# Latent-attention queries normed, split and projected between the last gate products; the sample recurrence in two buffers

## The chip, the cores and the metric

The kernel runs on one core of one Trainium2 chip. The metric is the time of one execution on the device in microseconds, here the median of three runs. The engines are TensorE (PE, matrix products; PEld is its weight load), VectorE (DVE), ScalarE (ACT), GpSimd (POOL) and SyncE (SP), which here only issues transfers.

## What is computed

One decoder layer on 1024 prompt tokens and 8 sample tokens (NT = 1032), width 1024. The input is modulated and projected once (`h @ w_in`); the columns feed a recurrence (RWKV-7), a latent attention (MLA) and two gates. The two branches are merged through the gates, then a norm and a layer of 64 routed experts follow. All of it is in float32. The part that the change touches:

```
h    = x * (1 + sc1) + sh1
proj = h @ w_in                  # 1792 rwkv | 384 q_low | 256 kv_low | 32 kr_low | 2048 gates
cq   = rmsnorm(q_low,  g_qnorm)
q    = (cq @ w_uq).reshape(b, t, 8, 64 + 32)
q_nope, q_rope = q[..., :64], rope(q[..., 64:], pos)
ckv  = rmsnorm(kv_low, g_kvnorm)          # an output too
k_rope = rope(kr_low, pos)                # one for all 8 heads, an output too
k_nope = ckv @ w_uk ; v = ckv @ w_uv      # per head
o_b  = causal softmax((q_nope k_nope + q_rope k_rope) * scale) v
# sample tokens, one step of the recurrence for each (state S, 8 heads of 64 x 64):
sa = S (-kk) ; S = S * w + sa (kk a)^T + v k^T ; o = S r
```

The last row of the rwkv columns of every sequence (`shift`) and the new S are outputs.

## The kernel before

Products in float32 are made of three: each operand is split in a hi part (a rounded copy, ScalarE) and a lo part (the rest, VectorE), and `mm3` issues hi x hi, lo x hi and hi x lo (lines 147 to 149). `split` (lines 1312 and 1315) makes the two parts. Activations lie with features on the partitions and tokens along the free axis, in chunks of 344 (`CH`).

The program is written with a tile framework: code order gives the dependences, pools with a number of buffers hold the tiles, and a scheduler puts the instructions on each engine in an order of its own that respects both. Each engine, and SP as a queue of transfers, goes through its list in order. An instruction that waits holds all behind it on its engine.

Around the change the stages are these.

1. `stage_b`, then `mla_in` (line 488): `win` projects 128 columns of `w_in` at a time, 72 products of 128x344 each, for q0, q1, q2, kv0, kv1 and kr. `mla_weights` (line 870) loads the rope tables, w_uq, w_uk and w_uv.
2. The gates. `gate` (line 331) projects 128 gate columns, writes them to DRAM (gateD) and adds four small `psada` products whose weights wada come in 1 MB loads. While g8 to g15 run, `mla_in` norms q and kv (square, a product with ones `psq`, root, reciprocal, scaling), and `rw_sample` (line 775) does the recurrence for the sample tokens: for four pairs of heads it loads the state sS and a broadcast of the inputs svb, both in one buffer and on POOL's queue, does nine VectorE steps and writes S back.
3. `mla_prep` (line 1050) in a pool of its own: `shift_out`, then the splits of the normed q (qp0 to qp2) and kv (kvp0, kvp1), w_uk and w_uv; `mla_rope` for two sets of four heads (products psqr; the halves of each head are swapped by a write to and a read from DRAM, swapD, and combined with the cosines and sines); `mla_k` (rope of the key, the ckv and krope rows by transposes psck); `mla_heads` for four pairs (q products psqn, k products pskn; each head's q and k as one 128-row tile, written to qD and kD); `mla_v` (psV, written to vD); `sample_queries` (psuk, psql, psqrs) and `rw_sample_rows` (psos).
4. `mla_prompt` (line 1086): for four pairs of heads it loads Va, and for each head qTa and kTa in one load each, and runs eight query tiles (sc scores, pspt transposes, pspv). The chunked recurrence of the prompt (`rwkv`) is interleaved with it. Output products, norm and experts follow.

Of the kernel before, what the change touches and what calls it, by code (L numbers as in the profile page):

```python
# [126 lines left out]
class Kern:  # L127
# [241 lines left out]
    def shift_out(self, pool):  # L369
        nc = self.nc  # L370
        so = pool.tile([9, 1792], F32, tag='ss', name='so', bufs=1)
        for g in range(4):
            n = min(4, 14 - g * 4)
            ps = self.ps(f'psso{g}')
            for j in range(n):
                self.tr(ps[:9, j * 128:(j + 1) * 128], self.plast[:, g * 4 + j, :])
            nc.scalar.activation(so[:, g * 512:g * 512 + n * 128], ps[:9, :n * 128], AF.Copy)
        nc.scalar.dma_start(self.O['shift_prompt'][0], so[0:1, :])
        nc.scalar.dma_start(self.O['shift_sample'][0], so[1:9, :])
# [108 lines left out]
    def mla_in(self, pool, keep):  # L488
        nc = self.nc
        T = lambda nm: keep.tile([128, NT], F32, name=nm)  # L490
        q = [self.win([(1792 + i * 128, 128)], f'q{i}', T(f'cq{i}')) for i in range(3)]
        kv = [self.win([(2176 + i * 128, 128)], f'kv{i}', T(f'ck{i}')) for i in range(2)]
        kr = self.win([(2432, 32), (2448, 16), (2432, 16)], 'kr', T('krraw'))
        self.epsr = self.cp.tile([128, 1], F32, name='epsr')
        nc.vector.memset(self.epsr, 1e-6)
        for tl, nm in ((q, 'g_qnorm'), (kv, 'g_kvnorm')):
            self.gate()
            rs = pool.tile([128, NT], F32, tag='rs', name='rs' + nm, bufs=1)
            sqs = []
            for t in tl:  # L500
                sq = pool.tile([128, NT], F32, tag='sq', name='sqm', bufs=3)
                nc.scalar.activation(sq, t, AF.Square)
                sqs.append(sq)
            for c0, n in CH:
                ps = self.ps('psq')
                for j, sq in enumerate(sqs):
                    nc.tensor.matmul(ps[:, :n], self.c('ones'), sq[:, c0:c0 + n], start=(j == 0), stop=(j == len(tl) - 1))
                nc.scalar.activation(rs[:, c0:c0 + n], ps[:, :n], AF.Sqrt, bias=self.epsr, scale=1.0 / (128 * len(tl)))
# [1656 lines left out]
def layer(tc, I, O, dbg=None):  # L2165
    nc = tc.nc
    with ExitStack() as ctx:
# [3 lines left out]
        with ExitStack() as b:  # L2171
# [14 lines left out]
            with sb('proj') as B:  # L2186
                K.stage_b(B)
# [111 lines left out]
```

## Time and profile before

| | us |
|---|---|
| median of 3 runs (2512.29 to 2514.46) | 2513.09 |
| the profiled execution | 2506.96 |
| its span | 2505.1 |
| stage 2, g8 to g15 with norms and sample recurrence | about 428 to 538 |
| stage 3, `mla_prep` | about 538 to 664 |
| stage 4, attention and prompt recurrence | about 664 to 1010 |
| TensorE busy over the span | 2165.5 (86%) |
| VectorE, ScalarE, GpSimd busy | 1422.0, 978.8, 972.0 |

Times in the rows are microseconds from the start of the span. The profile names tiles without their numbers: whg and wlg are the hi and lo parts of a gate's weights, g a gate, cq and ck the raw and then the normed q and kv columns. A row of the timeline is one instruction, or several of the same kind in sequence, with its start and its duration; matrix products overlap, so the step between two starts is the price of one, not the duration. The waits are given by who waited, for whom, the sum, the number and the longest.

### The profile page before, as it was taken

The numbers are of one execution on the slowest core, as the hardware profiler recorded it, in microseconds if no ns is written. First come the engines' busy times: TensorE is split into PE (matmuls) and PEld (weight loads), VectorE is DVE, ScalarE is ACT, GpSimd is POOL, SyncE is SP. The second block draws the span as 40 slices with busy tenths as digits, with TensorE's granted clock in tenths as the row PEclk, the third lists the DMA queues.
The fourth block names the chain that finished last, engine by engine and source line by source line (L and its number), as shares of the span: only waits on it lengthen the run. The fifth ranks groups of instructions, "written<-read, shape, count | busy, mean of one in ns | idle before, by whom it ended". The sixth has DMA issues, their size and how long they took to land. (4 is left out here: it accounts for less than half of the span.)

```text
span 2505.1 us, 39711 instructions
## 1 busy us (share of the span) xinstructions
PE 2165.5 (86%) x14376; PEld 1721.5 (69%) x14376; DVE 1422.0 (57%) x2637; ACT 978.8 (39%) x1722; POOL 972.0 (39%) x813
## 2 busy tenths in 40 slices
PE   4999999976799999799779688899999998799754
PEld 2898999865567878467768476576767767676331
DVE  1554441553476775554657865676666667575437
ACT  1433332322354454321326643444443444344325
POOL 2443340132300000320214765567576665565226
PEclk8999999987898999899899789899999999999877
DMA  8136662654551442654899669999999999899994
GB/s 281 45 79 173 178 185 56 181 160 135 199 161 32 147 128 73 246 192 135 278 236 226 146 154 273 317 310 323 326 307 313 308 303 340 245 312 292 319 316 159
DMA packets 353203, 537.86 MB, mean 215 GB/s; under 512 B 113467, under 2 KB 210178, under 8 KB 346652
## 3 DMA queue, kind: packets, MB, share of 16 engines
q1 hardware_dynamic: 288602, 415.90, 50.9%
q0 software_dynamic: 61520, 118.93, 19.9%
q8 instruction: 114, 1.87, 0.3%
q10 hardware_dynamic: 2882, 0.48, 0.1%
q14 instruction: 85, 0.70, 0.1%
HBM read 411.00 MB, written 124.77 MB: 214 GB/s over the span
## 5 line engine op out<-in xcount | busy, mean ns | idle before, releaser
L1794 POOL DMA_INDIRECT xg<-h2D,IG x303 | 353.3, 1166 | 242.1 <-DVE xt L1797 81.0
L1315 DVE TENSOR_TENSOR epl<-egu,eph 128x1024 fp32r<-128x1024 f32 x140 | 169.7, 1218 | 123.0 <-ACT eph L1312 122.6
L1312 ACT ACTIVATE eph<-egu 128x1024 fp32r<-128x1024 f32 x140 | 147.3, 1056 | 165.9 <-DMA egu<-in_w_exp_up_dram 102.7
L147 PE MATMUL psup<-xh,eph 128*128 128x360 f32 (+15 forms) x576 | 182.1, 325 | 21.9 <-ACT xh L1312 18.6
L149 PE MATMUL psup<-xh,epl 128*128 128x360 f32 (+15 forms) x576 | 178.3, 322 | 10.8 <-DVE epl L1315 10.0
L148 PE MATMUL psup<-xl,eph 128*128 128x360 f32 (+15 forms) x576 | 182.8, 320 | 4.0 <-DVE xl L1315 3.9
L1934 POOL DMA_INDIRECT accD<-ey,IS x65 | 115.2, 1773 | 112.8 <-ACT ey L1927 55.8
L147 PE MATMUL psy<-edh,ehh 128*128 128x512 f32 (+12 forms) x296 | 126.0, 432 | 23.7 <-ACT ehh L1312 11.4
L1315 DVE TENSOR_TENSOR edl<-ewd,edh 128x1024 fp32r<-128x1024 f32 x90 | 108.7, 1219 | 45.0 <-ACT edh L1312 44.3
L147 PEld LDWEIGHTS psup<-xh,eph 128*128 128x128 f32 x576 | 111.1, 195 | 31.7 <-ACT xh L1312 20.2
L1312 ACT ACTIVATE edh<-ewd 128x1024 fp32r<-128x1024 f32 x90 | 94.0, 1052 | 82.6 <-PE psy L149 67.2
L147 PE MATMUL pwg<-hh,whg 128*128 128x344 f32 x384 | 124.1, 323 | 0.0
L149 PEld LDWEIGHTS psup<-xh,epl 128*128 128x128 f32 x576 | 109.6, 194 | 19.9 <-DVE epl L1315 11.6
L148 PE MATMUL pwg<-hl,whg 128*128 128x344 f32 x384 | 122.6, 319 | 0.0
L149 PE MATMUL pwg<-hh,wlg 128*128 128x344 f32 x384 | 122.6, 319 | 0.0
L148 PE MATMUL psy<-edl,ehh 128*128 128x512 f32 (+12 forms) x296 | 120.9, 413 | 0.0
L148 PEld LDWEIGHTS psup<-xl,eph 128*128 128x128 f32 x576 | 111.5, 194 | 9.7 <-DVE xl L1315 5.4
L1797 DVE STREAM_TRANSPOSE xt<-xg 128x1024 f32<-128x1024 f32 (+3 forms) x61 | 113.9, 1873 | 0.2
L149 PE MATMUL psy<-edh,ehl 128*128 128x512 f32 (+12 forms) x296 | 109.9, 414 | 0.9 <-DVE ehl L1315 0.8
L1873 PE MATMUL psup<-xf,egu 128*128 128x176 f32 (+7 forms) x640 | 96.2, 304 | 2.7 <-DMA egu<-in_w_exp_gate_dram 2.1
L1873 PEld LDWEIGHTS psup<-xf,egu 128*128 128x128 f32 x640 | 91.6, 190 | 7.2 <-DMA egu<-in_w_exp_gate_dram 3.3
L1947 PE MATMUL psup<-egu,xf 128*32 128x128 f32 (+1 forms) x1024 | 77.1, 325 | 21.2 <-DMA egu<-in_w_exp_up_dram 16.9
(731 smaller groups left out, 5879.4 us busy)
## 6 DMA issues: line engine op xcount, KB each, us to landing
egu<-in_w_exp_gate_dram SPq DMA_DIRECT2D x256, 256.0 KB
egu<-in_w_exp_up_dram SPq DMA_DIRECT2D x256, 256.0 KB
ewd<-in_w_exp_down_dram SPq DMA_DIRECT2D x128, 512.0 KB
wada<-in_w_ada_dram SPq DMA_DIRECT2D x24, 1024.0 KB
accD<-zero SPq DMA_DIRECT2D x18, 512.0 KB
gateD<-g SPq DMA_DIRECT2D x16, 516.0 KB
bg<-gateD SPq DMA_DIRECT2D x48, 172.0 KB
wrg<-in_w_in_dram SPq DMA_DIRECT2D x16, 512.0 KB
```

What stands on the lines that cost most here:

```text
L147: nc.tensor.matmul(out, lh, rh, start=start, stop=False)
L148: nc.tensor.matmul(out, lh, rl, start=False, stop=False)
L149: nc.tensor.matmul(out, ll, rh, start=False, stop=stop)
L1312: nc.scalar.activation(hi, src, AF.Copy)
L1315: self.last_split = nc.vector.tensor_sub(lo, src, hi.bitcast(F32))
L1794: nc.gpsimd.indirect_dma_start(out=X[:, g, :], out_offset=None, in_=h4, in_offset=bass.IndirectOffsetOnAxis(ap=idx(j, g), axis=0))
L1797: nc.vector.transpose(out=dst.rearrange("p k (g b) -> p g k b", b=32), in_=X[:, 0:G, :].rearrange("p g (a k) -> p g k a", k=8))
L1873: nc.tensor.matmul(p[:, :C], gu[k // 2][:, j, k % 2, m * 128:(m + 1) * 128], xt[:, k, :C], start=(k == 0), stop=(k == 7))
L1934: self.nc.gpsimd.indirect_dma_start(out=acc, in_=y, in_offset=None, compute_op=OP.add, out_offset=bass.IndirectOffsetOnAxis(ap=idx, axis=0))
L1947: nc.tensor.matmul(ps[q * C:q * C + C, 0:2 * F].rearrange("p (a f) -> p a f", a=2), xt[:, k, :C], gu[k // 2][:, :, k % 2, q * F:q * F + F] ...
```

## The change

The banks of PSUM are split into five for the projections and three (`mq`) for the new work, after `stage_b`. The rest:

- `rw_sample` becomes `rw_sample_load` and one call for each pair of heads. sS and svb have two buffers. Their loads and the writes to sD go on SP's queue (they were on POOL's and ScalarE's). Pairs 0 and 1 are written between the q and the kv projections, 2 and 3 before g9.
- `mla_norm` goes by chunks of 344 and for q makes the hi and lo parts at once.
- `mla_rope`, `mla_q`, `mla_kr`, `mla_rows` and `shift_out` stand between g10 and g15. One pool of 8 buffers of 128x344 (tag `n`) serves all of them. The swap through DRAM is made for each chunk. Results go to DRAM as qnD (4 pairs of 128 rows), qrotD and krD. `shift_out` takes seven groups with 14 transfers on SP for two on ScalarE.
- `mla_prep` keeps the kv parts, kn and V and the sample queries. w_uk and w_uv are loaded there; they were loaded in stage 1.
- `mla_prompt` puts each head's q and k together from four loads: 64 rows of qnD, 32 of qrotD, 64 of knD, and the 32 rows of krD twice by a broadcast. 32 rows of q are set to zero by POOL.

```diff
...
+    def mla_in(self, qpool, keep, between):
...
+        self.mq = [self.win([(1792 + i * 128, 128)], f'q{i}', T(qpool, f'cq{i}')) for i in range(3)]
+        between()
+        self.mkv = [self.win([(2176 + i * 128, 128)], f'kv{i}', T(keep, f'ck{i}')) for i in range(2)]
+        self.mkr = self.win([(2432, 32), (2448, 16), (2432, 16)], 'kr', T(keep, 'krraw'))
...
+    def ntile(self, pool, nm):
+        return pool.tile([128, 344], F32, tag='n', name=nm, bufs=8)
+    def mla_norm(self, tl, nm, pool, parts=None):
+        nc = self.nc
+        for c0, n in CH:
+            s = slice(c0, c0 + n)
+            ps = self.ps('psq', 'mq')
             for j, t in enumerate(tl):
+                sq = self.ntile(pool, 'sqm')
+                nc.scalar.activation(sq[:, :n], t[:, s], AF.Square)
+                nc.tensor.matmul(ps[:, :n], self.c('ones'), sq[:, :n], start=(j == 0), stop=(j == len(tl) - 1))
+            rs = self.ntile(pool, 'rs' + nm)
+            nc.scalar.activation(rs[:, :n], ps[:, :n], AF.Sqrt, bias=self.epsr, scale=1.0 / (128 * len(tl)))
+            nc.vector.reciprocal(rs[:, :n], rs[:, :n])
+            for j, t in enumerate(tl):
+                nc.vector.scalar_tensor_tensor(t[:, s], t[:, s], self.v(nm, j), rs[:, :n], op0=OP.mult, op1=OP.mult)
+                if parts:
+                    self.split(parts[j][0][:, s], parts[j][1][:, s], t[:, s])
...
+    def rw_sample(self, hp, pool):
...
+        S = pool.tile([128, 8, 64], F32, tag='sS', name='sS', bufs=2)
+        V = pool.tile([128, 5, 8, 64], F32, tag='svb', name='svb', bufs=2)
+        for hh in range(2):
+            nc.sync.dma_start(S[hh * 64:hh * 64 + 64], I['state_wkv'][0, :, 2 * hp + hh].rearrange("b v k -> v b k"))
+            nc.sync.dma_start(V[hh * 64:hh * 64 + 64].rearrange("p j b k -> p (j b k)"),
+                              self.sD[hp, hh:hh + 1].rearrange("o j b k -> o (j b k)").to_broadcast([64, 2560]))
...
+        for hh in range(2):
+            nc.gpsimd.dma_start(self.O['wkv_sample'][0, :, 2 * hp + hh].rearrange("b v k -> v b k"), S[hh * 64:hh * 64 + 64])
...
     def orow(self, dt):
...
     def mla_rope(self, X, pool):
+            ps = self.ps('psqr', 'mq')
+            for k in range(3):
+                self.mm3(ps[:, :n], [w[:, k, X, :, :].rearrange("p a b -> p (a b)") for w in self.wqr],
+                         [t[:, s] for t in self.qp[k]], k == 0, k == 2)
+            t0, t1, t2 = [self.ntile(pool, f'qr{j}')[:, :n] for j in range(3)]
+            nc.scalar.activation(t0, ps[:, :n], AF.Copy)
+            nc.vector.tensor_mul(t1, ps[:, :n], self.cosT[:, s])
+            d = self.dr.tile([4, 4, 16, n], F32, name=f'swapD{X}{c0}')
             for j in range(2):
+                nc.sync.dma_start(d[:, 2 * j:2 * j + 2], t0)
+            nc.sync.dma_start(t2, d[:, 1:3])
+            nc.gpsimd.tensor_mul(t2, t2, self.sinT[:, s])
+            nc.gpsimd.tensor_add(t1, t1, t2)
+            nc.sync.dma_start(self.qrotD[X][:, s], t1)
+            if c0 + n == NT:
+                nc.gpsimd.tensor_copy(self.qrot[:, X, :], t1[:, NP - c0:])
+    def mla_q(self, hp, pool):
...
+        for c0, n in CH:
+            s = slice(c0, c0 + n)
+            ps = self.ps('psqn', 'mq')
+            for k in range(3):
+                self.mm3(ps[:, :n], [w[:, k, hp * 128:(hp + 1) * 128] for w in self.wqn], [t[:, s] for t in self.qp[k]],
+                         k == 0, k == 2)
+            t = self.ntile(pool, 'qn')[:, :n]
+            nc.scalar.activation(t, ps[:, :n], AF.Copy)
+            nc.sync.dma_start(self.qnD[hp][:, s], t)
+            if c0 + n == NT:
+                nc.gpsimd.tensor_copy(self.qS[:, hp, :], t[:, NP - c0:])
...
+        nc.sync.dma_start(self.krD, kr[0:32, 0:NP])
...
+    def mla_rows(self, gs, pool):
...
+        for g in gs:
+            n = 128 if g < 8 else 8
+            s = slice(g * 128, g * 128 + n)
+            ps = self.ps('psck', 'mq')
+            for j in range(2):
+                self.tr(ps[:n, j * 128:(j + 1) * 128], self.mkv[j][:, s])
+            self.tr(ps[:n, 256:288], self.mkr[0:32, s])
+            rw = self.ntile(pool, 'ckr')[:n, 0:288]
+            nc.vector.tensor_copy(rw, ps[:n, :288])
+            if g < 8:
+                nc.sync.dma_start(O['ckv_prompt'][0, 0, s, :], rw[:, 0:256])
+                nc.sync.dma_start(O['krope_prompt'][0, 0, s, :], rw[:, 256:288])
...
+    def mla_kn(self, hp, kv, pool):
...
         for c in range(2):
             s = slice(c * 512, c * 512 + 512)
             ps = self.ps('pskn')
             for j in range(2):
                 self.mm3(ps, [w[:, j, hp * 128:(hp + 1) * 128] for w in self.wuk2], [t[:, s] for t in kv[j]], j == 0, j == 1)
+            t = pool.tile([128, 512], F32, tag='kn', name='kn', bufs=2)
+            if c:
+                nc.scalar.activation(t, ps, AF.Copy)
+            else:
+                nc.vector.tensor_copy(t, ps)
+            nc.sync.dma_start(self.knD[hp][:, s], t)
...
+        self.wuk, self.wuv = [pool.tile([128, 2, 512], F32, name=nm) for nm in ('wuk', 'wuv')]
+        nc.sync.dma_start(self.wuk, I['w_uk'][0].rearrange("(k p) c -> p k c", p=128))
+        nc.sync.dma_start(self.wuv, I['w_uv'][0].rearrange("(k p) c -> p k c", p=128))
         def parts(nm, t):
+            p = [pool.tile(list(t.shape), F32R, name=nm + c) for c in 'hl']
             self.split(*p, t)
...
+        kvp = [parts(f'kvp{i}', t) for i, t in enumerate(self.mkv)]
+        self.wuk2 = parts('wuk', self.wuk)
+        self.mla_kn(0, kvp, pool)
+        self.wuv2 = parts('wuv', self.wuv)
         self.mla_v(kvp, pool)
+        for hp in range(1, 4):
+            self.mla_kn(hp, kvp, pool)
...
+                q = pool.tile([128, NT], F32, tag='qT', name=f'qTa{h}', bufs=2)
+                k = pool.tile([128, NP], F32, tag='kT', name=f'kTa{h}', bufs=2)
+                r, o = slice(e * 64, e * 64 + 64), slice(64 - e * 64, 128 - e * 64)
+                qd = QUAD.index(h % 4)
+                a, z = qd * 32, (qd ^ 1) * 32
+                nc.gpsimd.memset(q[z:z + 32, :], 0.0)
+                nc.sync.dma_start(q[r], self.qnD[hp, r])
+                nc.sync.dma_start(q[a:a + 32], self.qrotD[h // 4, a:a + 32])
+                nc.sync.dma_start(k[r], self.knD[hp, r])
+                nc.sync.dma_start(k[o], self.krD[None].to_broadcast([2, 32, NP]))
...
+            with ExitStack() as b, sb('qraw') as Q:
+                K.banks(b, mm=5, mq=3)
+                with sb('srw') as S:
+                    K.rw_sample_load(S)
+                    K.mla_weights(mw, S)
+                    K.page_rows(S)
+                    K.mla_in(Q, mw, lambda: [K.rw_sample(hp, S) for hp in range(2)])
+                    K.gate()
+                    for hp in range(2, 4):
+                        K.rw_sample(hp, S)
+                    K.gate()
+                K.mla_scratch(mwx.enter_context(sb('qp', 'right')))
+                with sb('norm', 'right') as N:
+                    K.mla_norm(K.mq, 'g_qnorm', N, K.qp)
+                    K.gate()
+                    K.mla_rope(0, N)
+                    K.mla_norm(K.mkv, 'g_kvnorm', N)
+                    K.gate()
+                    K.mla_q(0, N)
+                    K.mla_kr(N)
+                    K.mla_rope(1, N)
+                    K.gate()
+                    K.mla_q(1, N)
+                    K.shift_out(range(7), N)
+                    K.mla_rows(range(0, 5), N)
+                    K.gate()
+                    K.mla_q(2, N)
+                    K.mla_rows(range(5, 9), N)
+                    K.gate()
+                    K.mla_q(3, N)
                     K.gate()
...
```

How the instructions stand on the engines. TensorE before, the end of the last gate g15 (pwg) and what follows; psso is `shift_out`, psqr the first rope product, psck the ckv rows:

```order
L148 MATMUL pwg_4190<-hl,whg_4134 128x344
L149 MATMUL pwg_4190<-hh,wlg_4135 128x344
L229 MATMUL psada<-wada_4217,scT 32x512 x4
L163 MATMUL psso_4239<-CN_60,plast 9x128 x4
L163 MATMUL psso_4245<-CN_60,plast 9x128 x4
L163 MATMUL psso_4251<-CN_60,plast 9x128 x4
L163 MATMUL psso_4257<-CN_60,plast 9x128 x2
L147 MATMUL psqr<-qp0h,wqrh 128x344 x3
L163 MATMUL psck<-CN_60,ck_3051 128x128
L163 MATMUL psck<-CN_60,ck_3136 128x128
```

TensorE after, the same place:

```order
L148 MATMUL pwg_4714<-hl,whg_4658 128x344
L149 MATMUL pwg_4714<-hh,wlg_4659 128x344
L229 MATMUL psada<-wada_4741,scT 32x512 x4
L147 MATMUL pskn<-kvp0h,wukh 128x512
L148 MATMUL pskn<-kvp0l,wukh 128x512
L147 MATMUL pskn<-kvp0h,wukh 128x512
L148 MATMUL pskn<-kvp0l,wukh 128x512
L149 MATMUL pskn<-kvp0h,wukl 128x512
L147 MATMUL pskn<-kvp1h,wukh 128x512
```

Behind the last gate there now come the k products (pskn), whose wukh and wukl are parts of w_uk. A piece of g15 itself after, with the last pair's q products:

```order
L148 MATMUL pwg_4662<-hl,whg_4658 128x344
L147 MATMUL psqn<-qp0h,wqnh 128x344
L148 MATMUL psqn<-qp0l,wqnh 128x344
L149 MATMUL psqn<-qp0h,wqnl 128x344
L147 MATMUL psqn<-qp1h,wqnh 128x344
L148 MATMUL psqn<-qp1l,wqnh 128x344
L149 MATMUL psqn<-qp1h,wqnl 128x344
L147 MATMUL psqn<-qp2h,wqnh 128x344
L148 MATMUL psqn<-qp2l,wqnh 128x344
L149 MATMUL psqn<-qp2h,wqnl 128x344
L149 MATMUL pwg_4662<-hh,wlg_4659 128x344
```

The nine products of a chunk stand among those of the gate; before, they stood behind all gates. SP's queue before, ahead of the kv projections:

```order
L874 DMA rp<-in_rope_dram 128x2064
L876 DMA uqraw<-in_w_uq_dram 128x3x768
L888 DMA wuk<-in_w_uk_dram 128x2x512
L889 DMA wuv<-in_w_uv_dram 128x2x512
L314 DMA wrkv_3137<-in_w_in_dram 128x8x128
L314 DMA wrkr<-in_w_in_dram 128x8x32
L314 DMA wrkr<-in_w_in_dram 128x8x16 x2
L314 DMA wrg_3318<-in_w_in_dram 128x8x128
```

SP after, the end of the gates and the start of `mla_prep`:

```order
L337 DMA gateD<-g_4655 128x1032
L1068 DMA wuk<-in_w_uk_dram 128x2x512
L1069 DMA wuv<-in_w_uv_dram 128x2x512
L835 DMA osr<-oSD 128x32
L1100 DMA qTa_7060<-qnD 64x1032
L1101 DMA qTa_7060<-qrotD 32x1032
L1103 DMA kTa_7061<-krD 64x1x1024
L1100 DMA qTa_7067<-qnD 64x1032
L1101 DMA qTa_7067<-qrotD 32x1032
```

The loads of w_uk and w_uv have moved from the first place to the second, behind the write of the last gate, and the loads of the attention's first tiles stand right behind them. SP after, ahead of g8 to g10, the loads of the sample recurrence:

```order
L314 DMA wrkr<-in_w_in_dram 128x8x32
L314 DMA wrkr<-in_w_in_dram 128x8x16 x2
L807 DMA svb<-sD 64x2560 x2
L314 DMA wrg_3415<-in_w_in_dram 128x8x128
L806 DMA sS<-in_state_wkv_dram 64x8x64 x2
L807 DMA svb<-sD 64x2560 x2
L806 DMA sS<-in_state_wkv_dram 64x8x64 x2
L314 DMA wrg_3546<-in_w_in_dram 128x8x128
```

Before, SP held only the weight loads there, and the loads of svb and sS were on POOL's queue.

## Rows read from the trace of the kernel before

**Rows 1.** Busy time by stretch: PE, PEld, DVE, ACT, POOL, PEclk, DMA share, GB/s
```profile
405.00:538.00 133.00, 131.59 (x819) 118.32 (x819) 48.38 (x47) 32.53 (x54) 14.07 (x22) 1.00 0.57 157
538.00:664.00 126.00, 74.00 (x351) 62.31 (x350) 48.03 (x76) 33.51 (x56) 44.75 (x42) 0.76 0.48 159
664.00:1000.00 336.00, 330.76 (x3112) 256.02 (x3110) 225.93 (x754) 168.14 (x415) 23.77 (x36) 0.96 0.37 110
```

**Rows 2.** Waits of 538 to 665 us, TensorE's and one of ScalarE: total, times, longest
```profile
PE psV L147 <- DVE qT L981: 11.1, 1, 11.1
PE psqr L148 <- DVE qp0l L1315: 10.5, 1, 10.5
PE psqr L147 <- DVE ckr L911: 6.4, 1, 6.4
...
ACT V L958 <- DMA vD<-V: 28.0, 4, 22.9
```

**Rows 3.** VectorE's timeline at the recurrence's end; landing of svb's loads
```profile
546.09 0.69 DVE L803 TENSOR_TENSOR stmp<-sS,svb 128x512 f32<-128x512 f32 x1 [7.56 <-DMA sS<-in_state_wkv_dram]
552.24 1.22 DVE L1315 TENSOR_TENSOR qp0l<-cq,qp0h 128x1032 fp32r<-128x1032 f32 x1
...
DMA to landing us min/median/max: 7.4/7.4/7.4
```

**Rows 4.** TensorE's timeline, 512 to 661 us: start, duration, line, operation
```profile
512.68 0.43 PE L147 MATMUL pwg<-hh,whg 128*128 128x344 f32 x1
...
524.20 1.06 PE L229 MATMUL psada<-wada,scT 128*32 128x512 f32 x8
...
537.70 1.70 PE L163 MATMUL psso<-CN,plast 128*9 128x128 f32 x14
...
541.73 1.25 PE L163 MATMUL psck<-CN,ck 128*128 128x128 f32 x10
...
553.97 0.49 PE L149 MATMUL psqr<-qp0h,wqrl 128*128 128x344 f32 x1
...
555.98 0.49 PE L147 MATMUL psqr<-qp1h,wqrh 128*128 128x344 f32 x1
...
560.18 0.43 PE L148 MATMUL psqr<-qp2l,wqrh 128*128 128x344 f32 x1 [0.39 <-DVE qp2l L1315]
...
640.09 0.40 PE L147 MATMUL pskn<-kvp0h,wukh 128*128 128x512 f32 x1
...
642.63 0.40 PE L149 MATMUL pskn<-kvp1h,wukl 128*128 128x512 f32 x1
...
649.74 1.90 PE L1135 MATMUL psql<-qS,ukT 64*128 64x8 f32 x16 [5.84 <-ACT ukT L1126]
...
660.78 0.64 PE L1006 MATMUL sc<-kTa,qTa 128*128 128x128 f32 x2
```

**Rows 5.** ScalarE's timeline, a table load and a split
```profile
439.76 1.28 ACT L508 ACT_TABLE_LOAD   x1
...
540.06 1.05 ACT L1312 ACTIVATE qp0h<-cq 128x1032 fp32r<-128x1032 f32 x1
```

**Rows 6.** SP's timeline of the swap, and the stretch while its writes ran
```profile
571.45 1.21 SPq L945 DMA_DIRECT2D swapD<-qr  x2
...
587.21 0.58 SPq L946 DMA_DIRECT2D qr<-swapD  x1
...
580.00:587.00 7.00, 1.89 (x12) 1.60 (x11) 0.00 (x0) 0.00 (x0) 0.00 (x0) 1.00 0.30 103
```

**Rows 7.** Key loads: SP's issues, TensorE's first use, its waits from 664 on
```profile
652.93 0.47 SPq L1097 DMA_DIRECT2D kTa<-kD  x1
...
722.89 0.43 SPq L1097 DMA_DIRECT2D kTa<-kD  x1
...
727.62 0.39 PE L1006 MATMUL sc<-kTa,qTa 128*128 128x128 f32 x2
...
PE sc L1006 <- DMA kTa<-kD: 2.5, 2, 2.0
```

More of the change, by code (lines that the diff above doesn't have):

```diff
@@ L367, in shift_state, with shift_out @@
         self.plast = self.cp.tile([128, 14, 9], F32, name='plast')
-    def shift_out(self, pool):
+    def shift_out(self, gs, pool):
         nc = self.nc
[L371 to L379, printed above, removed]
+        for g in gs:
+            ps = self.ps(f'psso{g}', 'mq')
+            for j in range(2):
+                self.tr(ps[:9, j * 128:(j + 1) * 128], self.plast[:, g * 2 + j, :])
+            so = self.ntile(pool, 'so')[:9, 0:256]
+            nc.scalar.activation(so, ps[:9, :256], AF.Copy)
+            nc.sync.dma_start(self.O['shift_prompt'][0][:, g * 256:(g + 1) * 256], so[0:1, :])
+            nc.sync.dma_start(self.O['shift_sample'][0][:, g * 256:(g + 1) * 256], so[1:9, :])
     def stage_b(self, pool):
@@ L486, in stage_b @@
             nc.sync.dma_start(self.bvD[i], bv)
-    def mla_in(self, pool, keep):
-        nc = self.nc
[L490 to L508, printed above, removed]
-            nc.vector.reciprocal(rs, rs)
-            for j, t in enumerate(tl):
-                nc.vector.scalar_tensor_tensor(t, t, self.v(nm, j), rs, op0=OP.mult, op1=OP.mult)
-        self.mla_inputs = q, kv, kr
@@ new lines, in mla_weights, with mla_scratch @@
+                nc.gpsimd.tensor_copy(wqr[:, :, q, :], uq[:, h:8:4, 64:96])
+            self.split(*[w[:, k] for w in self.wqr], wqr)
+    def mla_scratch(self, pool):
+        F = lambda nm, shape: self.dr.tile(shape, F32, name=nm)
+        self.qnD, self.qrotD = F('qnD', [4, 128, NT]), F('qrotD', [2, 128, NT])
+        self.knD, self.krD, self.vD = F('knD', [4, 128, NP]), F('krD', [32, NP]), F('vD', [4, 128, 1024])
+        self.qS = self.cp.tile([128, 4, 8], F32, name='qS')
+        self.qrot = self.cp.tile([128, 2, 8], F32, name='qrot')
+        self.ckvS = pool.tile([8, 256], F32, name='ckvS')
+        self.qp = [[pool.tile([128, NT], F32R, name=f'qp{i}{c}') for c in 'hl'] for i in range(3)]
@@ new lines, in mla_kr @@
+    def mla_kr(self, pool):
+        nc = self.nc
+        kr = self.mkr
+        nc.gpsimd.tensor_mul(kr[0:32, :], kr[0:32, :], self.cosT[0:32, :])
+        for c0, n in CH:
+            s = slice(c0, c0 + n)
+            t2 = self.ntile(pool, 'krt')[0:32, :n]
+            nc.gpsimd.tensor_mul(t2, kr[32:64, s], self.sinT[32:64, s])
+            nc.gpsimd.tensor_add(kr[0:32, s], kr[0:32, s], t2)
+        nc.sync.dma_start(self.krD, kr[0:32, 0:NP])
+        self.kvS = self.cp.tile([128, 2, 8], F32, name='kvS')
+        for j in range(2):
+            nc.gpsimd.tensor_copy(self.kvS[:, j, :], self.mkv[j][:, NP:])
+        self.krS = self.cp.tile([32, 8], F32, name='krS')
+        nc.gpsimd.tensor_copy(self.krS, kr[0:32, NP:])
```

243 lines of the change are left out of this document (67 added, 176 removed).

## The prediction

> **What bounds the kernel now.** I read the busy time by stretch first, then TensorE's waits in the one stretch where it is idle, then the rows around that stretch. [rows 1]: from 405 to 538 us, while the gate products run, TensorE is busy 131.59 of 133 us at a granted clock of 1.00; VectorE is busy 48 us there, ScalarE 33. From 538 to 664, in `mla_prep`, it is busy 74.00 of 126 us, and its mean granted clock is 0.76. From 664 to 1000 (attention, with the prompt recurrence between) it is busy 330.76 of 336. So two stages are bound by TensorE itself, and between them 52 us of a 126 us stage are idle, a part of the rest at the lower clock. The idle time is no one thing: [rows 2] gives 11.1 us for a query tile whose buffer waits for its write to DRAM, 10.5 for the lo half of qp0, 6.4 for a ckv row tile, and eleven smaller ones. The 10.5 have a cause outside the stage: in [rows 3] VectorE sits 7.56 us until the last pair's state sS has come, does nine steps of 0.69 us, and only at 552.24 begins qp0l, which TensorE's second product needs. The first product of the attention starts at 660.78 [rows 4]. That time, and not the end of any one transfer, is what the change can move.
>
> **Moved between the gates.** The split and projection of the queries, the rope, the ckv rows and the shift rows leave the stage with the gaps and go into one that has none. In a stage that is full, they cost their whole time. [rows 4]: one gate's 72 products of 128x344 run from 512.68 to 524.20, 11.52 us, so 0.160 us each at full clock. The 18 rope and query groups of 9 are 162 products: 162 x 0.160 = 25.9 us. The 27 transposes for the ckv rows: ten took 1.25 us, so 3.4. The 14 of the shift rows 1.70. The norm's `psq` products were in this stage already. Sum 31.0 us, and the gates end at 537.70 + 31.0 = 568.7 if nothing stalls.
>
> What could stall there: (a) the norms. Their columns stay the same, but they go by chunks of 344, and ScalarE may change its table for each of the six chunks and back: at most eight more loads of 1.28 us [rows 5], 10 us of an engine that is busy 33 of 133. Three gates cover that. (b) The rotary swap through DRAM. The two writes of 1032 KB in all were issued at 571.45, the read at 587.21 when they had landed: 15.8 us [rows 6]; a third of the columns makes 5.3, with the read 8 or so (the read's landing is taken as half of the writes', from its half size). Six such chains lie over four gates of 12.5 us and their added products. But they stand on SP's queue in the order written, and behind them the next loads of wrg and wada. (c) The sample recurrence. Its loads now stand on SP between the weight loads, and its VectorE steps ahead of wlkv0, wlkv1, wlkr and wlg8, so TensorE's next projection waits if svb comes late: 7.4 us to landing [rows 3], nine steps of 0.69 us, one projection of some 12 us to cover them, and the two buffers let the next load start before. I count 3 us for all of it, between 0 and 10 (one late chain per two gates). Gates end at 571.7.
>
> **What is left of the prep.** wuk is now loaded after g15's gate has been written: the row on SP waits for ScalarE, whose last evacuation of the gate ended at the end of the gate's products. A load of 512 KB of this shape took under 4.7 us where the attention waited for one (issued 722.89, used 727.62), and 7.9 in the busy start of attention (652.93 to 660.78) [rows 4, 7]. I take 5, being nearer to the quiet one, since nothing else loads then. Then the hi split, 1.05 [rows 5], and the lo split, 1.22 [rows 3]: 7.3 us in which TensorE has nothing, after which it begins at the lower clock. In [rows 4] seven steps took 2.01 us (0.287 each) after the 10.5 us gap, against 0.160 at full clock, and the full steps came back from 560.18; half of those 6.7 us is the loss, 3.3. The 96 products of 128x512 (kn and V) at (642.63 - 640.09) / 11 = 0.231 us are 22.2. The sample queries' two psql groups of 1.90 [rows 4] follow, and by an estimate from their size another 2.3 for psqrs and psos, 6.1 us. Sum 7.3 + 3.3 + 22.2 + 6.1 = 38.9, and the first score product comes at 571.7 + 38.9 = 610.6: a gain of 50.2 against 660.78. From below: 31 us, if the lower clock costs nothing and the sample products find room in the run. From above 46, if the wuk load takes 7.9 and kn and V, which have two buffers each and wait for their writes, add 4: in the trace before ScalarE waited 28.0 us in all for V's writes [rows 2].
>
> TensorE's three waits in [rows 2] go with their causes: no query tile is held by a write in this stage, qp0l is split among the gates, the ckv rows are gone. What is late next is wuk.
>
> **What the attention pays.** Each head's keys were one load of 512 KB; they are now a load of 64 rows and one of krD, 32 rows read twice through a broadcast. Before, TensorE waited 2.5 us in all for kTa [rows 7], and the later of a pair had 4.7 us from issue to first use. The broadcast load is not in the trace. The nearest row is the swap's write with its outer dimension of 4: 1032 KB in 15.8 us, 65 KB per us, and over that stretch the DMA engines were 0.30 busy for 103 GB/s [rows 6]. At that rate 256 KB take 3.9 us and nobody waits; at half of it 7.8, and six loads after the first pair would be late by up to 3.1 us each, 19 in all. I take 5, since the order after leaves 24 to 74 TensorE rows between the last use of one key tile and the first of the next, against 23 to 60, and keep 0 and 19.
>
> The Trainium skill, "DMA: Bandwidth & Descriptors", section "Rules for kernel authors", says that a leading zero-stride broadcast of c copies confines the whole DMA to at most c engines, here two. For the swap, with its 4, the trace agrees: a share of 0.30 with other rows beside it. By the rule the broadcast goes at half the swap's rate, and the attention pays toward 19 rather than 5; that is the second rival.
>
> **The sum.** +31.0 and +3 in the gates, the stage behind them 38.9 in place of 660.78 - 537.70 = 123.1, +5 in the attention: 34.0 + 38.9 - 123.1 + 5 = -45.2. The scheduler also puts the rows of the recurrence and of the experts into another order; there is no row to price that, I allow 5 us either way. The profiled execution took 2506.96 us (span 2505.1), so 2461.8; the median of the three runs is 6.1 above it, 2513.09, so 2467.9.
>
> **Rivals.** (1) Everything is covered: no stall in the gates, 31 us for the prep, no wait for krD. -3 - 7.9 - 5 = -15.9 on the forecast: 2452. For it speaks that VectorE and ScalarE are idle over half of the gate stage; against it that wuk comes late, which the order shows. (2) The gain is partly given back: the two-copy loads of krD are late at each change of heads, 19 in place of 5, and the kn and V writes add their 4: 2467.9 + 14 + 4 = 2486. It decides where a krD load takes over 6 us. (3) Slower: SP's queue holds the gates. Each of the six swap chains waits on SP for its write to land, and the loads of wrg and wada behind it come after TensorE wants them. If each chain stood wholly in TensorE's way, 8 us x 6 = 48 us, the 45 are gone: 2467.9 + 48 = 2516 and slower. It decides from 7.5 us for each chain; against it, wada and wrg are issued over a gate ahead of use now, and TensorE waited only once for either in 133 us. (4) The change doesn't do what it says, the projections run behind the gates after all and the time stays at 2511 or so; the order after speaks against it, query products stand among gate products there.
>
> **How the numbers follow.** Forecast 0.62, rival 1 0.12, rival 2 0.18, rival 3 0.05, rival 4 0.03. A measurement of this kernel can tell 0.2%, 5 us, from no change. Faster by more: 0.62 + 0.12 + 0.18 = 0.92; within: 0.03; slower: 0.05. The range: below, rival 1 with 5 us for the order, 2447; above, rival 2 with 5 and 3 more for the stalls in the gates, 2494. That leaves out rivals 3 and 4 and some 0.1 at the ends.
>
> **What would show it.** Right: gates' products without gaps, TensorE's last psada at 569 to 579 us, one gap of 6 to 8 us before pskn with a lower clock behind it, the first sc at 602 to 618, waits of sc on kTa of 3 to 10 us. Wrong: waits of psqr, psqn or pwg on swapD's tiles, wlkv or whg (rival 3); waits of pskn on kn's write above 4 us, or of sc on krD's load above 15 (rival 2); a difference that lies behind 1000 us, in the experts, which no step here speaks of.

## The result and the profile after

The changed kernel took 2532.86 us in the median of 20 runs (2515.35 to 2549.38), the kernel before 2515.33 in the 20 beside them (2498.37 to 2534.97). The ratio is 1.0052, 95% interval 1.0027 to 1.0077: slower by half a percent, where 2468 us and a gain of 45 had been forecast. Runs of one kernel spread over some 35 us, much more than the first three of the kernel before let see, so the reading below goes by stages of the trace, and the times of kernels go by ratios of many runs.

The profiled execution after took 2533.37 us (span 2531.6). Three tiles of TensorE mark the stages. Each row gives the number of products, their shortest, median and longest duration in ns, and the first and last start: the last `psada` ends the gates, the first `sc` begins the attention, the last `pspv` ends it. Before:

```profile
L229 PE MATMUL psada<-wada,scT x192: 592/617/1062, 11.7 to 537.2; 128*32 128x512 f32 x192
L163 PE MATMUL pspv<-CN,rr x32: 272/328/476, 670.1 to 1012.7; 128*128 128x128 f32 x32
```

After:

```profile
L229 PE MATMUL psada<-wada,scT x192: 592/617/1063, 11.8 to 590.8; 128*32 128x512 f32 x192
L163 PE MATMUL pspv<-CN,rr x32: 283/328/476, 645.8 to 1021.3; 128*128 128x128 f32 x32
```

The first `sc` stood at 660.8 before [rows 4] and stands at 638.7 after. So 22 us are gained when the attention begins, and 9 are lost when it ends. The stages are those of the forecast, each with another size:

| us | before | after | change | forecast |
|---|---|---|---|---|
| end of the gates | 537.2, 538.3 | 590.8, 594.3, 593.5 | +55.1 | +34.0 |
| from there to the first sc | 123.6, 122.0 | 47.9, 47.4, 47.7 | -75.1 | -84.2 |
| first sc to last pspv | 351.9, 347.4 | 382.6, 375.2, 374.3 | +27.7 | +5 |
| last pspv to last psbr (sample attention, branch products) | 263.5, 261.8 | 268.8, 273.4, 270.0 | +8.1 | 0 |

The columns hold two profiles of the kernel before and three of the changed one, and the change is between their means. The four make +15.8 us. What lies behind them, up to the end of the span, differs by 21 us between the first two profiles of the changed kernel, and by 45 between the two of the kernel before, beside which its median was 2515 and 2548 us.

The stretches after, as in [rows 1] (PE, PEld, DVE, ACT, POOL busy; PEclk; DMA share; GB/s): the gates, the prep, the attention.

```profile
405.00:591.00 186.00, 171.41 (x1005) 150.66 (x1003) 55.19 (x72) 59.55 (x106) 26.53 (x33) 0.96 0.47 137
591.00:638.70 47.70, 31.63 (x149) 25.33 (x145) 10.53 (x22) 13.19 (x20) 8.73 (x13) 0.77 0.54 173
638.70:1022.00 383.30, 354.58 (x3205) 274.52 (x3205) 236.38 (x782) 174.75 (x429) 31.75 (x48) 0.91 0.35 97
```

The gates were full before (131.59 of 133) and now have 15 us of gaps; the attention was full (330.76 of 336) and now has 29. TensorE's waits after, first those of 400 to 640 us, then the largest of 640 to 1022 (total, times, longest):

```profile
PE pskn L147 <- ACT wukh L1320: 11.0, 1, 11.0
PE psq L509 <- ACT sqm L508: 7.0, 3, 3.7
PE psql L1143 <- ACT ukT L1134: 5.0, 2, 4.3
PE psso L163 <- ACT so L376: 4.0, 1, 4.0
PE psso L163 <- ACT qn L939: 3.6, 1, 3.6
...
PE sc L1020 <- DMA kTa<-krD: 23.5, 5, 6.3
```

The five waits in the gates are the three of psq and the two of psso, 14.6 us. None is for wrg, wada, whg or for the rope's own products. Where the first of them comes from is read across the engines:

```profile
472.09 1.23 SPq L921 DMA_DIRECT2D swapD<-qr  x2
...
480.19 0.55 SPq L922 DMA_DIRECT2D qr<-swapD  x1
480.83 1.09 SPq L921 DMA_DIRECT2D swapD<-qr  x2
489.69 0.54 SPq L922 DMA_DIRECT2D qr<-swapD  x1
...
489.74 0.87 ACT L508 ACTIVATE sqm<-ck 128x344 f32<-128x344 f32 x2 [9.09 <-DMA swapD<-qr]
...
490.29 0.96 PE L509 MATMUL psq<-sqm,CN 128*128 128x344 f32 x2 [3.73 <-ACT sqm L508]
...
495.04 0.92 POOL L923 TENSOR_TENSOR qr<-qr,rp 128x344 f32<-128x344 f32 x1 [7.25 <-DMA qr<-swapD]
```

ScalarE's square `sqm` needs one of the eight `n` buffers; the next one in turn holds a rope tile whose write to swapD has not landed. SP issues the second chunk's write only when the first one's has landed and its read is issued, since it goes through its list in order. The second chunk takes from 480.83 to 495.04, 14.2 us, until POOL has its data. ScalarE waits 9.09 us, and `psq`, which stands among the gate products on TensorE, waits 3.73 for ScalarE.

In the attention the waits are on krD. One stretch in the gates while only the swap runs, and two in the attention in which TensorE does nothing but wait for krD:

```profile
482.00:486.00 4.00, 4.00 (x28) 2.95 (x27) 0.00 (x0) 0.00 (x0) 0.12 (x1) 1.00 0.22 67
812.00:816.00 4.00, 0.00 (x0) 0.00 (x0) 0.32 (x1) 0.00 (x0) 0.00 (x0) 0.89 0.13 54
914.00:919.50 5.50, 0.00 (x0) 0.00 (x0) 0.21 (x2) 0.00 (x0) 0.00 (x0) 0.51 0.11 45
```

The DMA share is 0.13 and 0.11 there, about two engines of sixteen, at 54 and 45 GB/s; with the swap it is 0.22 and 67 GB/s, about four. The Trainium skill, "DMA: Bandwidth & Descriptors", section "Rules for kernel authors", says that an outermost dimension of size c below 16, as a leading broadcast of c copies is, keeps the whole transfer on at most c engines. The trace agrees, for krD with its 2 (0.11 to 0.13) and for the swap with its 4 (0.22). The granted clock falls in the gaps as well (0.51 in the last row). The loads of one change of heads, SP's issues and TensorE's first products with them:

```profile
901.00 0.54 SPq L1103 DMA_DIRECT2D kTa<-krD  x1
...
907.24 0.53 SPq L1103 DMA_DIRECT2D kTa<-krD  x1
...
912.98 0.46 PE L1020 MATMUL sc<-kTa,qTa 128*128 128x128 f32 x2 [2.64 <-DMA kTa<-krD]
...
919.77 0.77 PE L1020 MATMUL sc<-kTa,qTa 128*128 128x128 f32 x2 [6.28 <-DMA kTa<-krD]
```

From issue to use it is 12.0 and 12.5 us. Before, a load of twice the size had 4.7 at the quickest change of heads [rows 7]; where TensorE waited for it, it took longer, 8.6 us (issued 654.86, used 663.49) and 6.2 (903.70 and 909.89).

### The profile page after: what moved, and what is told of

Its sections match the earlier page's. It is cut to its first block, busy times and chain, and to the rows that moved or that the text cites. A ratio compares the mean times of both kernels' runs of the same rounds, so it can differ in the third digit from the quotient of the medians.

```text
span 2531.6 us, 39876 instructions
## 1 busy us (share of the span) xinstructions
PE 2191.4 (87%) x14376; PEld 1738.3 (69%) x14376; DVE 1402.9 (55%) x2638; ACT 981.8 (39%) x1740; POOL 952.9 (38%) x803
## 5 line engine op out<-in xcount | busy, mean ns | idle before, releaser
L1802 POOL DMA_INDIRECT xg<-h2D,IG x303 | 345.7, 1141 | 230.2 <-DVE xt L1805 101.5
L1942 POOL DMA_INDIRECT accD<-ey,IS x65 | 121.6, 1871 | 131.1 <-ACT ey L1935 55.5
L1020 PE MATMUL sc<-kTa,qTa 128*128 128x512 f32 (+3 forms) x192 | 89.6, 565 | 23.5 <-DMA kTa<-krD 23.5
```

The costliest lines, as they stand in the source:

```text
L1020: nc.tensor.matmul(ps[:, :n], qT[:, d:d + 128], kT[:, c0:c0 + n], start=True, stop=not last)
L1802: nc.gpsimd.indirect_dma_start(out=X[:, g, :], out_offset=None, in_=h4, in_offset=bass.IndirectOffsetOnAxis(ap=idx(j, g), axis=0))
L1942: self.nc.gpsimd.indirect_dma_start(out=acc, in_=y, in_offset=None, compute_op=OP.add, out_offset=bass.IndirectOffsetOnAxis(ap=idx, axis=0))
```

## The experiments

Theory: two transfers with a small outer dimension hold TensorE, krD's load at each change of heads, and the swap in the gates, through SP's order and the shared buffers. The prep has a third wait of its own. The rivals stand with each run. All but the two unchanged kernels are edits of the changed kernel. The second profile of the changed kernel and e1 to e3 shared one chip (kernel before 2513.67 us), e4 to e7 a second (2542.8), e8 and the last two profiles a third (2547.75), so only ratios are compared between them.

**krD in two loads.** 

> The changed kernel with one edit: the 32 rows of krD are loaded by two loads of 32 rows each in place of one load that reads them twice through a broadcast. Theory (the two-copy load is slow by itself): TensorE's waits for kTa, 23.5 us in the changed kernel, fall under 5, and the stretch from the first score product to the attention's last product falls from 383 us to 345 to 358, the kernel by 25 to 35 us, to about 0.993 of the time before. Rival (the loss comes from four loads for each head instead of two, or from the new order): one more load for each head makes it no better, the waits stay above 18 us and the stretch above 375.

```diff
-                nc.sync.dma_start(k[o], self.krD[None].to_broadcast([2, 32, NP]))
+                for z in range(2):
+                    nc.sync.dma_start(k[o][z * 32:z * 32 + 32], self.krD)
```

Ratio to the kernel before 0.9885 (0.9852 to 0.9919), against 1.0052 for the changed kernel. From the first sc (638.1) to the last pspv (986.0) it is 347.9 us, as before the change. The waits for kTa in 640 to 1000 us:

```profile
PE sc L1020 <- DMA kTa<-krD: 3.2, 2, 1.9
```

The theory holds: one more load for each head, and some 30 us less. Some 20 us of them are waits; the rest went with the lower clock, since the mean granted clock over the attention is 0.97 here and 0.91 to 0.94 in the three profiles of the changed kernel. The ratio moved by 1.7%, 42 us, and the 12 us beyond the attention's 30 are not accounted for.

**Rope tiles in the raw q columns.** 

> The changed kernel with one edit: the three tiles of a rope chunk no longer come from the pool of eight buffers but lie in the raw q columns, which are free by then. Theory (the rope's tiles hold the pool's buffers until their transfers land, ScalarE waits for a buffer, TensorE for ScalarE): the five stalls of TensorE between 486 and 549 us, 14.7 us, fall under 3, the gates end at 568 to 577 instead of 591. Rival (the swap through DRAM holds SP's queue and the weight loads or the banks behind it): the stalls move to other places of the gates and their end stays above 585.

```diff
-            t0, t1, t2 = [self.ntile(pool, f'qr{j}')[:, :n] for j in range(3)]
+            t0, t1, t2 = [t[:, s] for t in self.mq]
```

Ratio 1.0067 (1.0044 to 1.0090); the gates end at 592.2. The five stalls are gone, and one of 17.6 us is there instead:

```profile
PE psck L163 <- ACT so L376: 17.6, 1, 17.6
```

SP's and ScalarE's timelines show what moved:

```profile
507.37 5.50 SPq L921 DMA_DIRECT2D swapD<-cq  x4
...
530.54 6.62 SPq L925 DMA_DIRECT2D qrotD<-cq  x2
...
538.22 1.88 SPq L940 DMA_DIRECT2D qnD<-qn  x3
...
517.49 0.46 ACT L939 ACTIVATE qn<-psqn 128x344 f32<-128x344 f32 x1 [1.01 <-PE psqn L149]
...
545.47 0.86 ACT L376 ACTIVATE so<-psso 9x256 f32<-9x256 f32 x2 [21.63 <-DMA qnD<-qn]
```

The qn tiles were ready at 518 us and their write was issued at 538, behind a whole swap on SP; the buffers they held were those that `so` needed. The rival was right that the stalls would move and the gates end no earlier, but what stood behind the swap was the writes of qn, and not weight loads: with the rope's tiles out of the pool, SP's order still keeps the pool full.

**Late tiles ahead of the parts of kv.** 

> The changed kernel with one edit: in the prep pool the late tiles (ukT, qlT and eight tiles for kn in place of two) come ahead of the parts of kv, so that these no longer lie where the gates' tile badd was, which is written to DRAM at the end of the gates. Theory (kvp0l and kvp1h waited for that write until 600.3, and wukh stands behind kvp1h on ScalarE): the gap of TensorE behind the last gate, 11.0 us, falls to 5 to 8, and with the waits of kn for its two tiles gone the first score product comes 4 to 8 us earlier against the end of the gates (47.3 us after it in the changed kernel). Rival (the load of w_uk itself lands at 600): the gap stays at 10 to 12.

```diff
+        self.late = [pool.tile([128, 4, 256], F32, name='ukT'), pool.tile([128, 512], F32, name='qlT'),
+                     [pool.tile([128, 512], F32, name=f'kn{j}') for j in range(8)]]
...
-            t = pool.tile([128, 512], F32, tag='kn', name='kn', bufs=2)
+            t = self.late[2][2 * hp + c]
```

In the changed kernel the engines stood like this behind the last gate (POOL, VectorE, ScalarE):

```profile
592.47 2.09 POOL L255 DMA_DIRECT2D modD<-badd  x4 [10.85 <-DVE bd L1155]
...
600.28 1.23 DVE L1323 TENSOR_TENSOR kvp0l<-ck,kvp0h 128x1032 fp32r<-128x1032 f32 x1 [7.91 <-DMA modD<-badd]
...
590.81 1.05 ACT L1320 ACTIVATE kvp0h<-ck 128x1032 fp32r<-128x1032 f32 x1
600.34 1.06 ACT L1320 ACTIVATE kvp1h<-ck 128x1032 fp32r<-128x1032 f32 x1 [8.47 <-DMA qTa<-qnD]
601.31 1.04 ACT L1320 ACTIVATE wukh<-wuk 128x1024 fp32r<-128x1024 f32 x1
```

kvp0l and kvp1h lie where the gates' tile badd was, and wait until its write to DRAM has landed. The profile names qTa's load for kvp1h, but both begin together at 600.3. With the tiles elsewhere both are done by 601.7, though the gates end 5 us later and badd's last write is only issued at 599.3. So that write held both, and the releaser that is named need not be the one. wukh stands behind kvp1h. A second wait, 5.0 us of `psql` for ukT, comes from kn's two tiles: ScalarE waits for a tile's write to knD, and ukT stands right behind.

```profile
631.25 0.60 ACT L1005 ACTIVATE kn<-pskn 128x512 f32<-128x512 f32 x1 [3.40 <-DMA knD<-kn]
...
635.19 0.60 ACT L1005 ACTIVATE kn<-pskn 128x512 f32<-128x512 f32 x1 [2.86 <-DMA knD<-kn]
```

With the tiles elsewhere:

```profile
PE pskn L147 <- ACT wukh L1322: 6.2, 1, 6.2
```

From the gates' end (596.1) to the first sc (635.9) it takes 39.8 us instead of 47.7. The theory holds: the gap falls by 4.8, and psql's wait for ukT from 5.0 to 0.4, while other waits of 2.3 us and less come up. In this run wukh begins at 601.79, 5.2 us after the issue of wuk's load at 596.59, and now waits for that load. The kernel as a whole did not move by it that can be told, ratio 1.0049 (1.0029 to 1.0068).

**The swap on POOL's queue.** 

> The changed kernel with one edit: the three transfers of a rope chunk (the writes to swapD, the read back and the write to qrotD) are issued by POOL, which does the chunk's multiplications anyway, and no longer by SP. With the rope's tiles apart, the stalls only moved: one of 17.6 us at the ckv rows, where qn tiles ready at 515 to 517 us had their write issued at 538, behind the swap on SP. Theory (SP's order is what holds the buffers: each swap's wait keeps the writes of qn, so and g behind it): TensorE's stalls between the norm and the last gate, 14.7 us, fall under 4 and the gates end at 568 to 578 us instead of 591 to 594; the kernel gains 14 to 22. Rival (eight buffers are too few whatever the queue, since a chunk holds three of them over two slow transfers): the stalls stay above 10 us.

```diff
-                nc.sync.dma_start(d[:, 2 * j:2 * j + 2], t0)
-            nc.sync.dma_start(t2, d[:, 1:3])
+                nc.gpsimd.dma_start(d[:, 2 * j:2 * j + 2], t0)
+            nc.gpsimd.dma_start(t2, d[:, 1:3])
...
-            nc.sync.dma_start(self.qrotD[X][:, s], t1)
+            nc.gpsimd.dma_start(self.qrotD[X][:, s], t1)
```

Ratio 0.9997 (0.9964 to 1.0029). Two stalls of 9.3 us in all are left in the gates, 7.6 of them at psso, where ScalarE's qn again waits for a buffer:

```profile
PE psso L163 <- ACT qn L939: 7.6, 1, 7.6
PE psq L509 <- ACT sqm L508: 1.7, 1, 1.7
```

The last `psada` starts at 581.2, but the last query product, which now comes behind it, at 586.3, and the first sc at 632.6, 6 to 9 us ahead of the three profiles of the changed kernel. That is about half of the 14 to 22 expected. So SP's order is a part of the cause. A chunk still takes 12 to 17 us from the issue of its write to POOL's multiplication, and that the rest is this time in a shared pool is what the next run tests.

**The swap by rows.** 

> The changed kernel with one edit: the swap stays on SP, but is written once as 128 rows and read back by eight loads of 16 rows each, in place of two writes and one read whose outer dimension is 4. Theory (the swap's transfers are slow because few of the DMA engines carry them): from the issue of a write to POOL's multiplication, 11 to 14 us for a chunk in the changed kernel, it takes 5 to 8 us, and the stalls of the gates are under 8 us of 14.7. Rival (the time of a swap is latency and the waits on SP): eight loads cost SP more than they save, and the stalls stay at 12 us or more.

```diff
-            d = self.dr.tile([4, 4, 16, n], F32, name=f'swapD{X}{c0}')
-            for j in range(2):
-                nc.sync.dma_start(d[:, 2 * j:2 * j + 2], t0)
-            nc.sync.dma_start(t2, d[:, 1:3])
+            d = self.dr.tile([128, n], F32, name=f'swapD{X}{c0}')
+            nc.sync.dma_start(d, t0)
+            for j in range(8):
+                nc.sync.dma_start(t2[j * 16:j * 16 + 16], d[(j ^ 1) * 16:(j ^ 1) * 16 + 16])
```

Ratio 0.9943 (0.9906 to 0.9980). The gates have no stall left, and end at 572.3:

```profile
405.00:572.00 167.00, 167.00 (x1042) 152.16 (x1044) 59.90 (x80) 61.83 (x111) 27.07 (x35) 1.00 0.55 156
```

The first chunk, from the issue of its write to POOL:

```profile
478.53 0.33 SPq L920 DMA_DIRECT2D swapD<-qr  x1
482.48 3.57 SPq L922 DMA_DIRECT2D qr<-swapD  x8
...
487.91 0.92 POOL L923 TENSOR_TENSOR qr<-qr,rp 128x344 f32<-128x344 f32 x1 [48.80 <-DMA swapD<-qr]
```

The six chunks take 7.8 to 11.9 us, against 11.6 to 15.1 in the changed kernel: less was gained than the 5 to 8 expected, and it was enough. What shrank is the write, from 6.4 to 9.1 us between its issue and the read's to 1.9 to 4.0. So SP's order and the eight buffers do no harm when the writes are quick. The edit also writes the tile once where it was written twice; how much of it is the width and how much the halved write was not taken apart.

**The sample recurrence in one buffer.** 

> The changed kernel with the sample recurrence in one buffer for sS and svb and loaded on POOL's queue, as before, but at its new place between the projections. Theory (the second buffer lets the next pair's inputs land while the first is worked on; without it VectorE waits for svb with wlkv1, wlkr and wlg8 behind it): TensorE waits 5 to 25 us in the projections between 390 and 450, where it waited under 1. Rival (what matters is the early start alone, the projections are long enough to cover a load): no wait above 2 us, the time as that of the changed kernel.

Ratio 1.0086 (1.0053 to 1.0120), gates' end 595.9. In the projections TensorE is busy throughout, though VectorE now waits 32.1 us for sS there, against 16.2 for sS and svb together:

```profile
380.00:460.00 80.00, 80.00 (x506) 75.52 (x506) 34.56 (x49) 20.70 (x38) 19.52 (x31) 1.00 0.72 164
```

```profile
DVE stmp L810 <- DMA sS<-in_state_wkv_dram: 32.1, 3, 12.2
```

The rival is right: the early start alone takes the recurrence off the path. The second buffer hides waits that nobody waits for. The ratio is 0.0034 above the changed kernel's, about 9 us, which the two intervals do not tell from none.

**Three edits at once, and once more.** 

> The changed kernel with three edits: krD in two loads, the late tiles of the prep ahead of the parts of kv with eight tiles for kn, and the swap on POOL's queue. If the three losses are separate, they add up: attention 30 us, prep 5, gates 14 to 22, so that the time is 2460 to 2475 and the ratio to the kernel before 0.979 to 0.986, as was forecast for the change itself. Rival (they share a limit, so that what one gives another takes back): the time stays at the 2485 that two loads for krD gave alone.

e5 (e1, e3 and e4 together) gave 0.9846 (0.9798 to 0.9894), as expected. The better set has the swap by rows in place of POOL's queue:

> The changed kernel with the three edits that each did their part: the swap written and read by rows (gates end at 572 us instead of 591), krD in two loads (attention 348 us instead of 376 to 383), the late tiles of the prep ahead of the parts of kv (40 us from the end of the gates to the first score product instead of 47). If the losses are separate: gates end at 572, first score product at 610 to 614, last product of the attention at 958 to 966, and the time 0.976 to 0.984 of the kernel before. Rival (what is gained ahead of 1000 us is given back behind it): the stretch from the attention's last product to the first product of the expert lists, 424 us in the first profile of the kernel before, grows by 20 us or more and the ratio stays at 0.988 as with two loads alone.

Ratio 0.9776 (0.9730 to 0.9821). Gates' end 567.6, first sc 603.7, last pspv 953.2; 36.1 us of prep and 349.5 of attention. The three stages end 4 to 6 us ahead of what was expected. This is 2.2% faster than the kernel before (1.8 to 2.7%), and 2515 x 0.9776 = 2459 is close to what had been forecast for the change itself, though it takes three edits that the change did not have. The stretch from the last pspv to psek takes 459.5 us, 35 more than in the first profile of the kernel before, which was the rival's sign; but the kernel before takes 451.5 on this chip, so that little of it belongs to the edits. Its waits from 400 to 960 us:

```profile
PE pskn L147 <- ACT wukh L1323: 6.1, 1, 6.1
PE sc L1020 <- DMA kTa<-krD: 3.6, 2, 1.9
```

**The two kernels again.** 

> The kernel before as it is, a second profile, on the chip of the run before. The stretch from the attention's last product (1012.7 us) to the first product of psek took 424.3 us in its first profile, against 437.2 and 433.7 in the two of the changed kernel. If that difference belongs to the new order, it takes 422 to 427 here; if it is the spread of the transfers in that stretch, it takes 430 or more. The experts' products (psup, 967.5 us) differ by 5 us or more from run to run.

> The changed kernel as it is, a second profile. If the parts of the program up to the end of the attention are set by fixed waits, the gates end at 591 us, the first score product stands at 639 and the last product of the attention ends at 1022, each within 2 us of the first profile. What lies behind 1022 us took 1510 us in the first profile against 1492 before. If that difference is the spread of the experts' stage from run to run, it changes here by 5 us or more; if it belongs to the new order of instructions it stays at 1505 to 1515.

> The changed kernel as it is, on the same chip as the two others, for the table of stages: gates end at 590 to 595 us, first score product at 638 to 643, last product of the attention at 1016 to 1022, and from there to psek 432 to 438 us, if these belong to the order of instructions and not to the chip.

Ratios 0.9989 (0.9950 to 1.0027) for the kernel before against itself, 1.0047 (1.0016 to 1.0077) and 1.0060 (1.0019 to 1.0101) for the changed one. Up to the end of the attention each stage comes back within 1 to 8 us, as the table above has it, and not within the 2 us that were expected of the second profile. From the last pspv to psek it is 424.3 and 451.5 us before, 437.2, 433.7 and 455.5 after: that stretch as a whole goes by the chip and the run. Its first part, to the last psbr, does not: 262 to 264 before, 269 to 273 after, 276 in e8 and 280 in e6. That part takes 8 us more, or up to 18. Before and after:

```profile
1012.70:1276.20 263.50, 225.41 (x1717) 172.26 (x1715) 138.26 (x266) 72.32 (x143) 51.13 (x61) 0.93 0.68 227
1021.30:1290.10 268.80, 232.25 (x1717) 176.69 (x1715) 135.62 (x263) 72.88 (x143) 52.66 (x62) 0.91 0.66 222
```

TensorE has no more idle time there than before (38 and 37 us). The same number of products keeps it busy for 7 us longer, at a granted clock of 0.91 in place of 0.93, and of 0.89 in e6 and e8. Why the clock is lower there was not tried; the scheduler's other order of sample attention and branch products is a guess.

## Why the prediction was wrong

What was moved, what it costs in a stage that is full, and what it frees were right: with the swap's transfers widened, the gates end without a gap at 572.3 us in e6 and 567.6 in e8, where the products alone were to end at 568.7, and e8's first sc stands at 603.7, where 610.6 was forecast. The faults are the four small terms of the sum.

*What could stall in the gates*, 3 us of 0 to 10. Measured: 24, as 55.1 less the 31.0 of products; 14.6 of it waits, and some 7 by a granted clock of 0.96 over the stage, where it was 1.00 before and in e6. Two steps of (b) failed. A chunk's chain was priced at 8 us by dividing the unsplit swap by three; it took 14.2, 8.9 for the write where a third is 5.3, and 5.4 for the read where under 3 was taken: a third of the bytes took more than a third of the time. And the step asked who waits for the loads behind the swap on SP, and found wrg and wada early enough, which they were. It did not ask for the buffers: the rope's own writes to swapD and qrotD, and those to qnD and out_shift behind them on SP, give the eight buffers back, and ScalarE, which needs a buffer for sqm, qn and so, waits with TensorE behind it. (a) and (c) were right, and (c) more so than was needed.

*What is left of the prep*, 38.9 us. Measured 47.7, and 39.8 and 36.1 in e3 and e8. The products and their clock were priced right (31.6 us, and TensorE was busy 31.63). Of the 8.8 us more, 3.7 are the gap, 11.0 for 7.3, and 5.0 psql's wait for ukT, behind kn's writes. The order after showed wuk's late load, and the step stopped there; the parts of kv in the memory of badd were a later wait on another engine. "What is late next is wuk" is the sentence that failed: wuk was next but one. With the tiles elsewhere wukh waits for wuk, whose load took the 5 us that were counted. The wait for the writes of kn had been seen and priced, 4 us, but it stood in the upper end and in rival 2 and not in the sum.

*What the attention pays*, 5 us of 0 to 19. Measured 27.7, some 20 of it waits (20.1 to 23.9 in the three profiles, less 2.5 and 2.7 before) and the rest the lower clock. The mechanism had been told, with the rule and the price that follow from it, 7.8 us a load, and the price was about right: in the pair issued at 901.00 and 907.24 the second load came 6.8 us after the first. But from issue to use it was 12.0 and 12.5 us. The choice of 5 went by counts of TensorE rows between key tiles, and no row was priced: rows of an order have no time. The 4.7 us from issue to use [rows 7] was the quickest change of heads and not the usual one. The upper end counted each load by itself; it left out that the second load of a pair comes behind the first and that the clock falls behind each gap.

*Behind the attention*, 0 with 5 either way for the order. About 8 us are lost there, and the cause is open.

Rivals 2 and 3 were written as alternatives, at 2486 and 2516. They are two places of one cause, transfers with an outer dimension of 2 and 4, and both came in part (rival 3 by the buffers, and not by wrg and wada), with 9 us and 8 us more from two others. The range's upper end, 2494, did add something for all four terms (14, 4, 5 and 3). But each of the four came out above its own upper end: 24 for 10, 47.7 for 46, 27.7 for 19, 8 for 5. Even all four ends together, 7 + 7 + 14 + 5 = 33 us on the forecast, make 2501 and a faster kernel. So the ends themselves were too low: they were read from a larger transfer divided by three, and from loads that were counted one by one. The chance of slower, 0.05, was given to a chain that fails wholly, 48 us in one place, when 21, 9, 23 and 8 us more than assumed, in four places, were enough.

## What to carry to other kernels

A step that is moved into a full stage brings its transfers along, and what they hold (buffers of a shared pool, the queue's order) counts there as the products do: ask of each transfer how wide it is, and which buffers come free only when the ones behind it have been issued. Write no transfer with a broadcast or a small dimension outermost when someone waits for it; two loads of 32 rows were 30 us better than one of twice 32. And where several terms of a sum rest on one and the same guess, here on how fast a narrow transfer is, ask of each upper end whether it is one: an end that comes from dividing a larger transfer's time, or from the quickest case in the trace, is not.

## What the hardware showed that was not expected

- The load with two copies outermost ran at a DMA share of 0.11 to 0.13 and 45 to 54 GB/s, as the profile counts them, while TensorE waited for nothing else; the swap with 4 outermost at 0.22 and 67 GB/s.
- A gap of 4 to 6 us on TensorE costs more than itself. Behind the wait of 4.75 us that ends at 816.34 in the changed kernel, TensorE is busy without a pause and has a granted clock of 0.50 (1.2 GHz) for 17 us. The attention lost some 8 us more than its waits, and with krD in two loads (e1) both came back. The kernel before has such a stretch too, behind a wait of 1.92 us that ends at 743.11. After, then before:

```profile
817.00:834.00 17.00, 17.00 (x61) 12.07 (x60) 6.93 (x20) 1.93 (x8) 0.00 (x0) 0.50 0.00 1
745.00:760.00 15.00, 15.00 (x142) 9.78 (x142) 6.10 (x30) 4.84 (x13) 0.00 (x0) 0.50 0.15 18
```

- Runs of the same kernel differ by some 35 us. In the profiles the stages up to the attention's end come back within about 8 us; from psek to the last of the experts' products it is 968 to 980 us in the three profiles beside which the kernel before took 2513 to 2515 us, and 985 to 992 in the three of the third chip.
